# A two-layer hybrid kernel: retention by pairs of heads, and column sums that go through DRAM with each row in one piece

## The chip, the cores and the metric

The kernel runs on one core of a Trainium2 chip. The metric is the device time of one execution in microseconds. The engines spoken of are TensorE (PE in the profile, PEld its weight loads), VectorE (DVE), ScalarE (ACT), GpSimd (POOL), and SyncE (SP), which issues nearly all DMAs of this kernel in order from one queue.

## What is computed

Two models follow one another on a sequence of 512 positions of width 1024, each with two layers. Only the first model (block 1) holds code that is changed. One of its layers normalises the input, projects it, runs three branches (an RWKV-7 recurrence with 8 heads of 64, a retention with 4 heads, a spatial gating unit), gates and merges them, and ends with a gated feed-forward net. The parts of the reference that matter here:

```python
def retention_branch(p, cos, sin):
    q, k, v, g = jnp.split(p, ...)            # 4 heads, q and k of 64, v of 128
    q = rotary(q, cos, sin)
    k = rotary(k, cos, sin) * (RET_QK_DIM ** -0.5)
    ...
    y = (inner + cross)                       # (q k^T * decay) v, causal
    y = y * lax.rsqrt(jnp.mean(y * y, axis=-1, keepdims=True) + EPS)
    return y * jax.nn.silu(g)

def rwkv7_branch(...):
    ...
    kk = kk / jnp.maximum(jnp.sqrt(jnp.sum(kk * kk, axis=-1, keepdims=True)), 1e-12)
    y = rwkv7_scan(r, decay, k, v, kk, a)
    mean = jnp.mean(y, axis=-1, keepdims=True)
    var = jnp.mean(jnp.square(y - mean), axis=-1, keepdims=True)
    y = (y - mean) * lax.rsqrt(var + RW_GN_EPS) * lnx_g + lnx_b
    y = y + jnp.sum(r * k * r_k, axis=-1, keepdims=True) * v
    return y * g
```

## The kernel before, in words

Activations lie feature by position: a tile is 128 features by 512 positions. Each large product is done three times in a 32-bit round format (high times high, low times high, high times low, lines 170 to 172), so a tile of 128 outputs is 24 matmuls of 128x512. A weight block of 512 KB is loaded into one of two buffers (wraw, L157), split by ScalarE (whi, L161) and VectorE (wlo, L162) into one of two buffers each. The product gathers in one of two PSUM banks of pool pm, and VectorE takes it out (L428 in block 1). Pool pw has four banks (function P) for the chains of the recurrence, pool pf has two (function PF).

In a layer of block 1 the order of TensorE's work is written by a planner (class Plan, functions step and run). Threads are Python generators that issue instructions and then yield a step. Dense(cost) and TILE (cost 1.4) are dense work: the projections, six matmuls at a time, of thread rwkv_in (rank 1), then branches (retention, then the gating unit; rank 2), then gates1, the 24 gate tiles (rank 3), which fill whatever is left. Chain(cost, wait) says that the thread's next step is due after so many units of planned time, counted on all costs issued, and comes before dense work then. When nothing is left to issue, planned time jumps ahead. The orders of the other engines are made by the scheduler of the framework; within "with self.late()" an operation stands behind the last evacuation that was issued.

The chains around the change:

- rw_pair (one for each two heads f of the recurrence): psw and psa, two 64-row products (L477, L479); the squares of k are summed over each head (sums, "psk"), and after Chain(0.4, 13.0) kkr is made with the result (L527), then kr, bd (L530 to L533); psbon; after a further wait psA (L546) uses bd.
- rwkv_inverse on VectorE (L570 to L586), then two lanes of units (rw_unit) which work through four f and four chunks g; unit f > 1 is not begun until rw_final of f-2 has ended.
- rw_final: six small steps psz, then the sums "psmean" and, after Chain(0.4, 10.0), y plus mean (L742), "psq", Chain(1.6, 11.0), y times its norm (L755) and the last products (L756 to L758); the result is yrw[f].
- retention, for each pair f: q, k (with a rotation), v, and then for each head e of the pair in turn: a gate tile gt, the decay table dec by DMA (L800), and four steps j with a score of 512 - 128 j columns (pssc, L807; 64 rows of q and k: rows 0 to 63 for e = 0, 64 to 127 for e = 1), its product with the decay (pret, L810, VectorE) and psret (L812), which gathers the four. Both pssc and psret are in pool pf. After each head "psrn" sums its squares (norms), and ret_end multiplies (L825) when Chain 12.0 has passed.

The helper sums (L198 on) sums a tile over partitions for four chunks of 128 positions at once, into rows 32 g + i of a 128x128 tile (g the chunk, i the head of n), writes that whole tile to DRAM (sumd, L207, 64 KB) and reads it back n times (L209), each read a broadcast of one row, in four pieces of 128 numbers, to 128/n partitions.

After the plan the merge runs: for each tile of pbr a gate is read from DRAM (L934), the three branches are projected in the order of merge_order, VectorE multiplies (L940) and adds (L944). The first tile that uses yrw is the fifth.

Of the kernel before, what the change touches and what calls it, by code (L numbers as in the profile page):

```python
# [10 lines left out]
F32 = mybir.dt.float32  # L11
# [7 lines left out]
S = 512  # L19
# [36 lines left out]
def Chain(cost, wait):  # L56
    return Step(cost, wait, chain=True)
# [49 lines left out]
class Kern:  # L107
# [90 lines left out]
    def sums(self, x, sel, n, ps, out, fn):  # L198
# [7 lines left out]
        d = self.dp.tile([4, 32, 128], F32, name="sumd", tag="sumd", bufs=8)  # L206
        nc.sync.dma_start(d.rearrange("g r t -> (g r) t"), t)  # L207
        for i in range(n):
            nc.sync.dma_start(out[i * 128 // n:(i + 1) * 128 // n, :].rearrange("p (g t) -> p g t", g=4),  # L209
                              d[:, i][None].to_broadcast([128 // n, 4, 128]))  # L210
# [259 lines left out]
    def rw_pair(self, l, f, r, k, vt, m, lora, half):  # L470
# [52 lines left out]
        yield Chain(0.4, 13.0)  # L523
# [74 lines left out]
    def lane(self, l, i):  # L598

        while self.units:  # L600
# [9 lines left out]
            if not self.left[f]:  # L610
                self.plan.add(self.rw_final(l, f, self.states[f]), 0, 2.0)
# [98 lines left out]
    def rw_final(self, l, f, st):  # L710
# [6 lines left out]
        yield Chain(0.0, 1.0)  # L717
# [22 lines left out]
        yield Chain(0.4, 10.0)  # L740
# [12 lines left out]
        yield Chain(1.6, 11.0)  # L753
# [15 lines left out]
    def retention(self, l, win):  # L769
# [4 lines left out]
        for f in range(2):  # L774
# [18 lines left out]
            ws = self.stream([win[l, 22 + 2 * f], win[l, 23 + 2 * f]])  # L793
            for e in range(2):
                h = 2 * f + e
# [4 lines left out]
                dec = F(name="dec"); nc.sync.dma_start(dec, I["c_dec1"][h])  # L800
                yield Chain(0.0, 1.0)
                hs = slice(64 * e, 64 * e + 64)
                psy = self.PF(name="psret")
                for j in range(4):
                    n = S - 128 * j
                    ps = self.PF(name="pssc")
                    nc.tensor.matmul(ps[:, :n], lhsT=qk[1][hs, j * 128:(j + 1) * 128], rhs=qk[0][hs, j * 128:],  # L807
                                     start=True, stop=True)
                    p = T(name="pret")
                    nc.vector.tensor_tensor(p[:, :n], ps[:, :n], dec[:, :n], op=OP.mult)  # L810
                    yield Chain(0.3 + n / 1024, 3.2)
                    nc.tensor.matmul(psy[:, j * 128:], lhsT=vt[j // 2][:, j % 2, e * 128:(e + 1) * 128], rhs=p[:, :n],  # L812
                                     start=(j == 0), stop=(j == 3), skip_group_check=True)
                y = self.tile("Y", name="yret")
                sq = T(name="sqr")
                nc.scalar.activation(sq, psy, AF.Square)
# [1326 lines left out]
```

## Time and profile before

| | us |
|---|---|
| median of 3 runs | 3266.28 (3265.93 to 3267.68) |
| profiled execution | 3264.7 |
| its span, first to last instruction | 3263.0 |
| TensorE busy in the span | 3208.0 |
| VectorE busy | 2187.2 |
| ScalarE busy | 1362.0 |

The mean granted clock of TensorE is 0.996 of full speed. A busy time of TensorE counts each matmul from its start to a modelled end; they overlap in a pipeline, so that the distance between two starts is shorter than one's duration, and it is the distance that adds up to the span. A 32-bit matmul ("f32" with a 128x128 or 64x512 input that isn't split) stands in the profile as two records.

The first mixing stage of block 1 lies at about 20 to 500 us of the span with its merge from 487, the second at about 975 to 1450 with its merge from 1439.

### The profile page before, as it was taken

Reading aid. Unit: us, or ns where it says so; the run is one execution under the profiler, and the core shown is the slowest. Engines: PE = TensorE matmul, PEld = TensorE weight load, DVE = VectorE, ACT = ScalarE, POOL = GpSimd, SP = SyncE. Lnnn points to the kernel's source line nnn. Section 1 sums busy time; section 2 is a strip of 40 time slices with the busy share of each in tenths; the row PEclk is TensorE's granted clock in tenths of the full one; section 3 lists DMA queues with packets and bytes.
Section 4 is the critical chain, followed back from the end, with each engine's and each line's share of the span. In section 5 each row is a group of like instructions: output and inputs, shape, how many; then the busy total and the mean of one; then the engine's idle time right before and its main releaser. Section 6 shows DMA issues by size and latency. Waiting matters only on the chain.

```text
span 3263.0 us, 47497 instructions
## 1 busy us (share of the span) xinstructions
PE 3208.0 (98%) x17992; PEld 2574.7 (79%) x17992; DVE 2187.2 (67%) x4071; ACT 1362.0 (42%) x2442; POOL 124.9 (4%) x176
## 2 busy tenths in 40 slices
PE   8999999999999999999999999999999999999998
PEld 6787877888887787878888887877788888777777
DVE  6875656777537855656677456987666669866665
ACT  5533434444335333434444334344334443443343
POOL 0000000000000000000000000010003100100031
PEclk9999999999999999999999999999999999999999
DMA  4433245433433423245333436453355564534464
GB/s 148 132 99 88 85 137 178 127 102 97 139 107 108 130 82 96 81 156 180 101 97 98 150 122 206 143 148 109 118 194 187 175 174 139 152 109 124 151 213 145
DMA packets 199797, 434.75 MB, mean 133 GB/s; under 512 B 29833, under 2 KB 58633, under 8 KB 199569
## 3 DMA queue, kind: packets, MB, share of 16 engines
q1 hardware_dynamic: 197904, 429.62, 42.8%
q8 instruction: 142, 2.33, 0.3%
q0 software_dynamic: 512, 1.05, 0.1%
q10 hardware_dynamic: 1152, 1.05, 0.1%
q14 instruction: 87, 0.70, 0.1%
HBM read 339.05 MB, written 61.36 MB: 123 GB/s over the span
## 4 chain that ended last, share of the span: by engine, by line
PE 82%; DVE 8%; DMA 6%; issue 2%; ACT 2%; SPq 0%; POOL 0%; DVEq 0%; ACTq 0%; POOLq 0%
PE pm L170 21%; PE pm L172 21%; PE pm L171 21%; PE psy L1186 2%; PE pbr L170 2%; PE pbr L171 2%; PE pbr L172 2%; PE pspt L1176 2%; DVE wlo L162 2%; DMA rdw<-sumd 1%; DMA sqr<-sumd 1%; PE psl L1158 1%; PE psl L1159 1%; DMA sqk<-sumd 1%; DMA sumd<-sums 1%
## 5 line engine op out<-in xcount | busy, mean ns | idle before, releaser
L170 PE MATMUL pm<-shi,whi 128*128 128x512 f32 x3064 | 1227.0, 400 | 0.9 <-ACT whi L161 0.9
L172 PE MATMUL pm<-shi,wlo 128*128 128x512 f32 x3064 | 1202.2, 392 | 1.4 <-DVE wlo L162 1.4
L171 PE MATMUL pm<-slo,whi 128*128 128x512 f32 x3064 | 1201.0, 392 | 0.0
L161 ACT ACTIVATE whi<-wraw 128x1024 fp32r<-128x1024 f32 x480 | 508.4, 1059 | 887.0 <-PE pm L171 527.6
L162 DVE TENSOR_TENSOR wlo<-wraw,whi 128x1024 fp32r<-128x1024 f32 x480 | 588.1, 1225 | 198.4 <-ACT whi L161 193.1
L170 PEld LDWEIGHTS pm<-shi,whi 128*128 128x128 f32 x3064 | 577.3, 188 | 138.4 <-issue 26.9
L172 PEld LDWEIGHTS pm<-shi,wlo 128*128 128x128 f32 x3064 | 576.6, 188 | 125.8 <-DVE wlo L162 4.0
L171 PEld LDWEIGHTS pm<-slo,whi 128*128 128x128 f32 x3064 | 577.5, 188 | 111.7 <-issue 4.1
L428 DVE TENSOR_TENSOR ev<-pm,rb 128x512 f32<-128x512 f32 x138 | 94.7, 687 | 110.9 <-PE pm L172 110.1
L897 DVE TENSOR_TENSOR gate<-pm,rb 128x512 f32<-128x512 f32 x80 | 55.0, 688 | 127.3 <-PE pm L172 127.0
L170 PE MATMUL pbr<-shi,whi 128*128 128x512 f32 x288 | 113.8, 395 | 1.1 <-DVE gate L940 0.8
L170 PE MATMUL pm<-whi,shi 128*128 128x256 f32 x384 | 112.5, 293 | 1.3 <-DVE ev L428 1.3
L171 PE MATMUL pbr<-slo,whi 128*128 128x512 f32 x288 | 112.2, 390 | 0.0
L172 PE MATMUL pbr<-shi,wlo 128*128 128x512 f32 x288 | 112.2, 389 | 0.0
L171 PE MATMUL pm<-wlo,shi 128*128 128x256 f32 x384 | 108.9, 284 | 0.6 <-DVE wlo L162 0.6
L172 PE MATMUL pm<-whi,slo 128*128 128x256 f32 x384 | 108.9, 284 | 0.0
L940 DVE SCALAR_TENSOR_TENSOR gate<-gate,pbr 128x512 f32<-128x512 f32 x128 | 85.7, 683 | 29.1 <-PE pbr L172 28.5
L944 POOL TENSOR_TENSOR gate<-gate 128x512 f32<-128x512 f32 x48 | 78.0, 1626 | 590.5 <-DVE gate L940 335.6
L937 ACT ACTIVATE gate<-gate 128x512 f32<-128x512 f32 x128 | 76.2, 625 | 46.0 <-DMA gate<-gtd 40.1
L1143 ACT ACTIVATE p<-psl,st 128x256 f32<-128x256 f32 (+3 forms) x128 | 65.1, 512 | 60.4 <-DVE st L1141 50.9
L170 PEld LDWEIGHTS pm<-whi,shi 128*128 128x128 f32 x384 | 73.6, 192 | 3.8 <-DVE ev L428 1.7
L171 PEld LDWEIGHTS pm<-wlo,shi 128*128 128x128 f32 x384 | 73.8, 192 | 1.3 <-DVE wlo L162 1.1
(524 smaller groups left out, 4401.8 us busy)
## 6 DMA issues: line engine op xcount, KB each, us to landing
wraw<-in_w_gt SPq DMA_DIRECT2D x148, 512.0 KB, 3.6
wraw<-in_w_in SPq DMA_DIRECT2D x116, 512.0 KB, 3.6
wraw<-in_f_up SPq DMA_DIRECT2D x88, 512.0 KB, 3.5
gtd<-gate SPq DMA_DIRECT2D x116, 256.0 KB, 2.0
gate<-gtd SPq DMA_DIRECT2D x116, 256.0 KB, 4.2
wraw<-in_w_br SPq DMA_DIRECT2D x44, 512.0 KB, 3.7
wraw<-in_f_dn SPq DMA_DIRECT2D x44, 512.0 KB, 3.5
wraw<-in_w_out SPq DMA_DIRECT2D x32, 512.0 KB, 3.7
```

Source lines behind the costliest of these rows:

```text
L161: nc.scalar.activation(hi[:, :n], raw[:, :n], AF.Copy)
L162: nc.vector.tensor_tensor(lo[:, :n], raw[:, :n], hi[:, :n].bitcast(F32), op=OP.subtract)
L170: nc.tensor.matmul(ps, lhsT=lhs[0], rhs=rhs[0], start=first, stop=False, skip_group_check=skip)
L171: nc.tensor.matmul(ps, lhsT=lhs[0], rhs=rhs[1], start=False, stop=False, skip_group_check=skip)
L172: nc.tensor.matmul(ps, lhsT=lhs[1], rhs=rhs[0], start=False, stop=last, skip_group_check=skip)
L428: self.last = self.nc.vector.tensor_tensor(t, ps, self.rb, op=OP.mult)
L937: nc.scalar.activation(g, g, AF.Tanh, scale=0.5)
L940: nc.vector.scalar_tensor_tensor(g, g, 1.0, pb, op0=OP.add, op1=OP.mult)
L944: (nc.gpsimd if self.pre and n in self.cfg.get("pa", (1, 2, 3)) else nc.vector).tensor_tensor(g, g, acc[c], op=OP.add)
L1143: nc.scalar.activation(p[:, :w], l, AF.Exp, bias=st[:, 0:1], accum_out=st[:, 1:2])
L1176: nc.tensor.transpose(pt_[:, b * 128:(b + 1) * 128], ps[e][:, b * 128:(b + 1) * 128], self.ident)
L1186: nc.tensor.matmul(psy[64 * e:64 * e + 64, :], lhsT=vs[e][b], rhs=pts[e][:, b * 128:(b + 1) * 128], start=first and b == 0, stop=last and ...
```

## The change

Three things are changed together. In sums each row of the result gets a DRAM tile of its own, [4, 128], so there is one small write (4 partitions of 512 B) and one read (a broadcast of 2 KB in one piece) for each row i. In retention the two heads of a pair are worked together: both gate tiles first, then each step j has the scores of both heads one behind the other, both products with the decay, and in the next step both psret. The scores move from pool pf to pool pw, and so does psrn; dec moves from tag F to tag Y. The planned waits of some chains are other ones.

```diff
         t = self.ap.tile([128, 128], F32, name="sums", tag="sums", bufs=2)
         fn(t, ps)
-        d = self.dp.tile([4, 32, 128], F32, name="sumd", tag="sumd", bufs=8)
-        nc.sync.dma_start(d.rearrange("g r t -> (g r) t"), t)
+        d = self.dp.tile([n, 4, 128], F32, name="sumd", tag="sumd%d" % n, bufs=8)
         for i in range(n):
-            nc.sync.dma_start(out[i * 128 // n:(i + 1) * 128 // n, :].rearrange("p (g t) -> p g t", g=4),
-                              d[:, i][None].to_broadcast([128 // n, 4, 128]))
+            nc.sync.dma_start(d[i], t[i:128:32, :])
+        for i in range(n):
+            nc.sync.dma_start(out[i * 128 // n:(i + 1) * 128 // n, :],
+                              d[i].rearrange("g t -> (g t)")[None].to_broadcast([128 // n, S]))
...
-        yield Chain(0.4, 13.0)          # rw_pair, before kkr
+        yield Chain(0.4, 15.0)
...
-                self.plan.add(self.rw_final(l, f, self.states[f]), 0, 2.0)
+                self.plan.add(self.rw_final(l, f, self.states[f]), 0, 2.5)
...
-        yield Chain(0.0, 1.0)           # rw_final, before psz
+        yield Chain(0.0, 2.5)
...
-        yield Chain(0.4, 10.0)          # rw_final, behind psmean
+        yield Chain(0.4, 7.5)
...
-        yield Chain(1.6, 11.0)          # rw_final, behind psq
+        yield Chain(1.6, 8.5)
...
+            gts, decs = [], []
             for e in range(2):
-                h = 2 * f + e
                 gt = self.evac((yield from self.fm_steps(ws)), "F")
                 th = T(name="th")
                 nc.scalar.activation(th, gt, AF.Tanh, scale=0.5)
                 nc.vector.scalar_tensor_tensor(gt, th, 1.0, gt, op0=OP.add, op1=OP.mult)
-                dec = F(name="dec"); nc.sync.dma_start(dec, I["c_dec1"][h])
-                yield Chain(0.0, 1.0)
-                hs = slice(64 * e, 64 * e + 64)
-                psy = self.PF(name="psret")
-                for j in range(4):
-                    n = S - 128 * j
-                    ps = self.PF(name="pssc")
-                    nc.tensor.matmul(ps[:, :n], lhsT=qk[1][hs, j * 128:(j + 1) * 128], rhs=qk[0][hs, j * 128:],
+                dec = self.tile("Y", name="dec"); nc.sync.dma_start(dec, I["c_dec1"][2 * f + e])
+                gts.append(gt); decs.append(dec)
+                yield TILE if not e else Chain(1.4, 1.0)
+
+            psy = [self.PF(name="psret") for _ in range(2)]
+            for j in range(4):
+                n = S - 128 * j
+                ps = [self.P(name="pssc") for _ in range(2)]
+                for e in range(2):
+                    hs = slice(64 * e, 64 * e + 64)
+                    nc.tensor.matmul(ps[e][:, :n], lhsT=qk[1][hs, j * 128:(j + 1) * 128], rhs=qk[0][hs, j * 128:],
                                      start=True, stop=True)
-                    p = T(name="pret")
-                    nc.vector.tensor_tensor(p[:, :n], ps[:, :n], dec[:, :n], op=OP.mult)
-                    yield Chain(0.3 + n / 1024, 3.2)
-                    nc.tensor.matmul(psy[:, j * 128:], lhsT=vt[j // 2][:, j % 2, e * 128:(e + 1) * 128], rhs=p[:, :n],
+                p = [T(name="pret") for _ in range(2)]
+                for e in range(2):
+                    nc.vector.tensor_tensor(p[e][:, :n], ps[e][:, :n], decs[e][:, :n], op=OP.mult)
+                yield Chain(0.4 + n / 600, 3.6)
+                for e in range(2):
+                    nc.tensor.matmul(psy[e][:, j * 128:], lhsT=vt[j // 2][:, j % 2, e * 128:(e + 1) * 128], rhs=p[e][:, :n],
                                      start=(j == 0), stop=(j == 3), skip_group_check=True)
+            sqs, ys = [], []
+            for e in range(2):
                 y = self.tile("Y", name="yret")
                 sq = T(name="sqr")
-                nc.scalar.activation(sq, psy, AF.Square)
-                nc.vector.scalar_tensor_tensor(y, psy, 0.5, gt, op0=OP.mult, op1=OP.mult)
-                yield Chain(0.4, 3.0)
-                self.norms(sq, self.sel[:, 1], 1, self.PF([128, 128], "psrn"), bias=self.eps[:, 0:1], scale=1.0 / 128)
-                self.plan.add(self.ret_end(l, h, y, sq), 0, 12.0)
-                yield Dense(0.4)
+                nc.scalar.activation(sq, psy[e], AF.Square)
+                nc.vector.scalar_tensor_tensor(y, psy[e], 0.5, gts[e], op0=OP.mult, op1=OP.mult)
+                sqs.append(sq); ys.append(y)
+            yield Chain(0.8, 4.0)
+            for e in range(2):
+                self.norms(sqs[e], self.sel[:, 1], 1, self.P([128, 128], "psrn"), bias=self.eps[:, 0:1], scale=1.0 / 128)
+                self.plan.add(self.ret_end(l, 2 * f + e, ys[e], sqs[e]), 0, 10.0 + e)
+            yield Dense(0.8)
```

The words behind # in the five lines of planned waits are added here to say where each stands.

## Rows read from the trace of the kernel before

**Rows 1.** The page, first part: busy us of each engine, share, instructions.
```profile
PE 3208.0 (98%) x17992; PEld 2574.7 (79%) x17992; DVE 2187.2 (67%) x4071; ACT 1362.0 (42%) x2442; POOL 124.9 (4%) x176
```

**Rows 2.** Stretches: length, busy PE, PEld, DVE, ACT, POOL; PEclk, DMA share, GB/s.
```profile
20.00:500.00 480.00, 469.83 (x3317) 369.75 (x3316) 312.33 (x582) 200.96 (x410) 0.87 (x1) 1.00 0.35 108
975.00:1450.00 475.00, 465.87 (x3293) 367.02 (x3292) 308.62 (x572) 198.15 (x407) 0.63 (x1) 1.00 0.36 106
```

**Rows 3.** TensorE's waits, whole span: who waits for whom: total us, times, longest.
```profile
PE pbr L170 <- DVE gate L940: 6.6, 4, 2.9
PE psA L546 <- DVE kkr L533: 5.6, 5, 1.8
PE psam L651 <- ACT rhs L635: 3.6, 4, 1.2
...
PE psret L812 <- DVE pret L810: 2.3, 3, 1.0
```

**Rows 4.** Timeline of TensorE around scores: start, us, operation, shapes [idle before].
```profile
136.99 0.39 PE L172 MATMUL pm<-shi,wlo 128*128 128x512 f32 x1
...
137.67 0.39 PE L172 MATMUL pm<-shi,wlo 128*128 128x512 f32 x1
137.98 1.12 PE L807 MATMUL pssc<-ev 64*128 64x512 f32 x2
139.04 0.50 PE L170 MATMUL pm<-shi,whi 128*128 128x512 f32 x1
139.37 0.39 PE L171 MATMUL pm<-slo,whi 128*128 128x512 f32 x1
...
150.57 0.81 PE L812 MATMUL psret<-pret,vret 128*128 128x384 f32 x2
151.31 0.70 PE L807 MATMUL pssc<-ev 64*128 64x256 f32 x2
151.94 0.50 PE L170 MATMUL pm<-shi,whi 128*128 128x512 f32 x1
```

**Rows 5.** Timeline of TensorE at two 64-row products, psw and psa.
```profile
45.32 0.39 PE L172 MATMUL pm<-shi,wlo 128*128 128x512 f32 x1
45.64 0.69 PE L477 MATMUL psw<-mix,lora 64*128 64x512 f32 x1
45.65 0.69 PE L479 MATMUL psa<-mix,lora 64*128 64x512 f32 x1
...
46.70 0.50 PE L170 MATMUL pm<-shi,whi 128*128 128x512 f32 x1
```

**Rows 6.** The page's DMA issues: count, KB each, median us to landing.
```profile
sqr<-sumd SPq DMA_DIRECT2D x8, 256.0 KB, 8.3
...
rdw<-sumd SPq DMA_DIRECT2D x16, 128.0 KB, 5.7
...
cumb<-cumd SPq DMA_DIRECT2D x8, 256.0 KB, 3.7
```

**Rows 7.** Timeline of SyncE's queue behind the last psq of the first layer.
```profile
489.50 0.32 SPq L207 DMA_DIRECT2D sumd<-sums  x1
492.10 1.24 SPq L209 DMA_DIRECT2D rdw<-sumd  x2
```

**Rows 8.** Timeline of VectorE at the first layer's merge.
```profile
499.69 0.69 DVE L755 TENSOR_TENSOR y<-y,rdw 128x512 f32<-128x512 f32 x1 [4.33 <-DMA rdw<-sumd]
500.30 0.68 DVE L940 SCALAR_TENSOR_TENSOR gate<-gate,pbr 128x512 f32<-128x512 f32 x1
```

**Rows 9.** Timeline of TensorE at the same place.
```profile
501.13 0.63 PE L170 MATMUL pbr<-shl,whi 128*128 128x512 f32 x1 [2.91 <-DVE gate L940]
...
504.85 0.39 PE L170 MATMUL pbr<-shi,whi 128*128 128x512 f32 x1
```

**Rows 10.** The stretch 502 to 504, columns as in rows 2.
```profile
502.00:504.00 2.00, 2.00 (x6) 1.62 (x5) 1.93 (x4) 1.73 (x3) 0.00 (x0) 0.50 0.00 0
```

**Rows 11.** Timeline of VectorE at one kkr.
```profile
128.77 0.75 DVE L527 SCALAR_TENSOR_TENSOR kkr<-mix,vec,sqk 128x512 f32<-128x512 f32 x1 [3.30 <-DMA sqk<-sumd]
```

## The prediction

> **What bounds the kernel now.** I read the page's first part first: TensorE is busy for 3208.0 of 3263.0 us, VectorE for 2187.2 [rows 1]. So only two things can shorten this kernel: less TensorE time, or less of the 55 us in which it waits. Everything the change touches lies in block 1, which runs twice, so I next read the table of stretches for the two mixing stages: TensorE is busy 469.83 of 480 us and 465.87 of 475 us, VectorE about 65% of them [rows 2]. That leaves 10.2 + 9.1 us of idle time in these stages; cutting waits there can win no more. Third, the list of who waits for whom on TensorE [rows 3]: the largest named waits that belong to block 1 are psA on the last product of kkr (5.6 us in 5), psam on ACT L635 (3.6 in 4), psret on pret (2.3 in 3), and two of the four waits of pbr (2.9 us each, one at each layer's merge). The main term must therefore come out of TensorE's own time, and for that the timeline of TensorE must be read start to start: a busy TensorE isn't at its peak, and only the distance between starts tells what an instruction costs.
>
> **Scores by pairs.** Dense 128x512 matmuls start 0.227 us apart (136.99 to 137.67 in three steps). A score of 512 columns uses 64 of the 128 rows: the last dense start before it is at 137.67, it starts at 137.98, the next dense at 139.04 and the one after at 139.37 [rows 4]. So it takes 1.06 us, plus 0.08 before it (0.31 in place of 0.227) and 0.10 behind it (0.33 in place of 0.227): 1.24 us. The score of 256 columns behind a psret takes 151.94 - 151.31 = 0.63, and the psret of 384 columns before it takes 0.74, where 384 columns at the score's slope are 0.645: again 0.10 before and 0.10 behind [rows 4]. The slope is (1.06 - 0.63) / 256 = 1.68 ns a column, which gives 0.84 for 384 and 0.41 for 128 columns. With 0.18 to 0.20 for the two changes of shape the four scores of a head cost 1.24 + 1.03 + 0.83 + 0.60 = 3.70 us, of which about 2.13 is columns and 1.57 switching.
>
> What do two of them cost together? The trace of before has the very case: psw (rows 0 to 63) and psa (rows 64 to 127), both 64x512 in fp32, both into banks of the same pool. They start at 45.64 and 45.65, and the next dense matmul starts at 46.70: 1.06 us for both, with the same 0.32 before them [rows 5]. The second is free. In the changed kernel heads e=0 and e=1 stand on just these halves, and their two scores are issued in one loop with nothing between. So one of two heads' scores vanishes: 3.70 us for each pair, 2 pairs in a layer, 2 layers, **14.8 us**. The psret matmuls use all 128 rows and don't pair; their count is unchanged. Bounds: 8.5 if only columns are saved (4 x 2.13) and 15.5 if the norms, two of which now also share a place, save a switch as well (4 x 0.18).
>
> The Trainium skill (TensorEngine Tiling (Array Packing), Key Properties) says that tiles of different rows run in parallel and that a change of mode drains TensorE; both agree with these rows. The same page (Gotcha 1: PSUM Pressure) warns that row tiling needs more banks, and that speaks against this change; it is a rival below.
>
> **Banks of PSUM.** Today a score goes into pool pf (2 banks, with psret), and the recurrence's chains have pw (4 banks) to themselves. After, psret holds both pf banks for a whole pair, and the pairs of scores and psrn take pw. The trace shows what a wait for a bank of pw costs: psam on L635, 3.6 us in 4, 0.9 each [rows 3]. Of the 16 pairs of scores the 8 of f=1 run among the chains; if each met one such wait, 7.2 us; if none did, 0, and the four of now may also go. I take **2.5 us lost**, a third, because a score's bank is read by one VectorE instruction of 0.7 us or less and VectorE is a third idle.
>
> **psret and its decay table.** The planned wait goes from 3.2 to 3.6 for two products instead of one. Each pret stays one VectorE instruction; psret of e=0 (0.74 us for 384 columns, [rows 4]) covers that of e=1. The table of e=1 is fetched as late as today's, so one wait of 1 us in each pair may stay: between 2.3 us won [rows 3] and 1.7 lost (4.0 in place of 2.3); I take 0.
>
> **The sums through DRAM.** Today one 64 KB write and then, for two rows, two reads in pieces of 512 B. The reads land after 5.7 (rdw) and, with one row, 8.3 us (sqr); cumb, a broadcast of one 2 KB row to 128 partitions, moves as many bytes as sqr and lands after 3.7 [rows 6]. The new form is cumb's. I take 3.7 in place of 5.7 to 8.3, with 0 saved and 4.6 saved as ends. The write of a sum with two rows becomes two small ones, which costs SyncE one more issue of 0.32 us [rows 7] ahead of the weight loads that queue behind it. I take it at nothing: the two weight buffers stand for a tile of 24 dense matmuls, 24 x 0.227 = 5.5 us, ahead of TensorE, and the reads, 0.62 us to issue now [rows 7], have a quarter of the pieces; without that cover it would be 0.3 us a sum. The Trainium skill (DMA: Bandwidth & Descriptors, Specifications) puts line rate at 512 B and above; by that sentence alone the reads would gain nothing. The trace disagrees as far as it shows, 3.7 against 8.3.
>
> What this is worth is read where somebody waits for it.
> (a) *The merge.* VectorE sits from 495.4 to 499.69 in front of y L755 for rdw's read, and L940, which would free a bank of pm, is queued behind it until 500.30 [rows 8]. TensorE stops 2.91 us [rows 9], and then runs at half clock: granted 0.50 in 502 to 504, the level of 1.2 GHz [rows 10]. From 501.13 to 504.85 there are nine distances of matmuls, 3.72 us where 9 x 0.227 are 2.04 [rows 9]. So the stall costs 2.91 + 1.68 = 4.6 us, and the second layer has its twin: 9.2. After: writes issued at 489.5 and 489.8 land near 492.4, as the one of now has by 492.1 [rows 7]; reads issued by 492.8 land at 496.5; y to 497.2, L940 to 497.9, and the fifth tile was to start at about 498.06. Moreover psq itself comes earlier against the dense work: the planned waits behind mean and norm fall by 2.5 each (10 to 7.5, 11 to 8.5) while two grow by 0.5 and 1.5, and the gate tiles of retention now count 2.8 in the plan where they counted 0. So gates are left to fill the time behind psq. I take the whole **9.2 us**; ends 0 and 9.2.
> (b) *psA.* kkr is late because VectorE waits 3.30 us for sqk's read [rows 11]. The read comes some 2 us sooner and the planned wait is 2 longer; the longest wait of TensorE here is 1.8 [rows 3]. Of 5.6 us I take **4.5**; ends 0 and 5.6.
> (c) The shorter waits of rw_final (7.5, 8.5) and ret_end (10, 11 instead of 12) let VectorE reach y before the data, as now. Among dense tiles two banks and the same two weight buffers cover that for 5.5 us; without this cover it is the stall under (a), 4.6 us each. Nothing is taken.
>
> **Sum.** 14.8 + 9.2 + 4.5 - 2.5 = 26.0 us. The profiled execution took 3264.7 (span 3263.0), so 3238.7; the median of the runs, 3266.28, is 1.6 above it: 3240.3, and I say 3240. Edits that leave the number of ACT and VectorE instructions as it is (the decs in tag Y, the lists, the order of th and gt) cost nothing: VectorE has 35% to spare.
>
> **Rivals.**
> 1. *The reads don't get faster.* VectorE then waits at the merge as before, (a) is 0 and (b) gets only its two planned units, say 2: 14.8 + 2 - 2.5 = 14.3, 3252. For it: the reads queue behind 512 KB weight loads, which this change leaves alone. Against: cumb's 3.7 [rows 6]. This is the case that the Trainium skill's sentence on 512 B would give.
> 2. *PSUM pressure.* Each f=1 pair waits for a bank (7.2) and psA's wait stays: 14.8 + 9.2 - 7.2 = 16.8, 3249. For it: two of four pw banks go at once while two lanes use the pool. Against: in 955 us only 3.6 us of such waits [rows 2, 3].
> 3. *The pair doesn't overlap.* Then only 16 x 0.39 of switching is saved, 6.2, the sum 17.4, 3249. Rows 5 speak against it.
> 4. *Slower:* the scores of both heads wait on banks that VectorE frees late, because it sits in front of a sum's read. One stop of 2.9 us costs 4.6 with the half clock [rows 9]. Of 16 pairs 7 would have to stop so (32 us) to eat the 28.5 of (a), (b) and the scores; all 16 would give 3266 + 74 - 28.5, but 9, the likely lot if lanes and sums coincide, 41, give 3279. For it: TensorE's order is fixed, so a late bank stops all; against: no stop among the chains is now above 1.8 us.
>
> **How the numbers follow.** Forecast 0.65 (3232 to 3247); rival 1 0.13; rival 2 0.09; rival 3 0.03; rival 4 0.05; a mixture in which little is left (planned order worse for the chains) 0.05. Upper end of the gain: 15.5 + 9.2 + 5.6 + 2.3 = 32.6, 3233; lower: 8.5 + 4.6 - 7.2 = 6, 3260. The range 3231 to 3256 takes in rivals 1 to 3 and leaves out rival 4 and part of the mixture. A measurement of this kernel can tell about 0.2%, 6.5 us, from no change: faster by more 0.89, within 0.06, slower 0.05.
>
> **What would show it.** In the new profile pssc of e=0 and e=1 start within 0.02 us and the next dense start follows 1.06 us (512 columns) later; the reads of sumd land in about 4 us; no wait of pbr near 2.9 and no stretch at 0.50 behind it; psA's waits under 1.5 us in all. The prediction is wrong if pairs of pssc start one behind the other, or if new waits of pssc, psh or psu for banks add up to more than 8 us.

## The result, and the profile after

The changed kernel takes 3234.34 us (median of 4 runs, 3233.67 to 3236.9) against 3266.98 of the kernel before on the same chip: ratio 0.9898, 95% interval 0.988 to 0.9915. The profiled execution took 3233.67 us with a span of 3232.0, so 31.0 us less than that of before. The forecast of 3240 had the size nearly right, but, as the experiments show, two of its terms were off by more than 10 us each, in opposite directions.

The page of the changed kernel, busy time of the engines, beside [rows 1]:

```profile
PE 3185.4 (99%) x17992; PEld 2567.0 (79%) x17992; DVE 2184.4 (68%) x4071; ACT 1359.0 (42%) x2438; POOL 124.9 (4%) x176
```

TensorE is busy 22.6 us less; the rest of the 31.0 is idle time that has gone. Its waits in the changed kernel, beside [rows 3] (who waits for whom, total us, times, longest):

```profile
PE psam L653 <- ACT rhs L637: 2.9, 4, 1.3
PE psam L653 <- DVE y L760: 2.6, 2, 1.4
...
PE psz L724 <- DVE cc L726: 2.3, 2, 1.2
...
PE pbr L170 <- DVE gate L951: 1.8, 2, 1.2
PE psz L724 <- DVE am L658: 1.7, 1, 1.7
PE psA L548 <- DVE kkr L535: 1.6, 4, 0.5
...
PE psmean L202 <- DVE am L658: 1.1, 2, 0.6
```

pbr fell from 6.6 to 1.8 us, psA from 5.6 to 1.6, and psret isn't in the list any more. The two stops of 2.9 us at the merges of block 1 are gone altogether: what is left of pbr stands at 3085 us and later, in the second model, whose code is the same in both kernels. New or longer are the lines of the recurrence: psam on y, psz and psmean make, together with pst (1.2) and psam on rhs (3.6 before), 11.8 us. VectorE's waits for rows of sums are listed next, first before (50.2 us in all), then in the changed kernel:

```profile
DVE y L755 <- DMA rdw<-sumd: 19.9, 6, 4.3
...
DVE yret L825 <- DMA sqr<-sumd: 12.2, 4, 6.4
...
DVE y L742 <- DMA cc<-sumd: 9.8, 4, 4.0
...
DVE kkr L527 <- DMA sqk<-sumd: 8.3, 6, 3.3
```

```profile
DVE yret L836 <- DMA sqr<-sumd: 1.7, 2, 1.2
DVE y L744 <- DMA cc<-sumd: 1.5, 2, 1.0
```

TensorE around two pairs of scores (start, us, operation), beside [rows 4]. The first group has the scores of both heads and nothing else:

```profile
140.46 1.13 PE L812 MATMUL pssc<-ev 64*128 64x512 f32 x4
141.52 0.50 PE L170 MATMUL pm<-shi,whi 128*128 128x512 f32 x1
...
152.62 1.45 PE L819 MATMUL psret<-pret,vret 128*128 128x384 f32 x4
154.00 0.70 PE L812 MATMUL pssc<-ev 64*128 64x256 f32 x4
154.63 0.50 PE L170 MATMUL pm<-shi,whi 128*128 128x512 f32 x1
```

Four records (two matmuls of 512 columns) take 141.52 - 140.46 = 1.06 us, exactly what one took before. Two of 256 columns take 0.63, as one did.

The first layer's merge: all engines, only the steps of the chain of the last psq, beside [rows 7 and 8]:

```profile
468.85 0.43 PE L202 MATMUL psq<-rdw,sel 128*32 128x128 f32 x8
...
470.72 1.10 SPq L209 DMA_DIRECT2D sumd<-sums  x2
472.97 1.14 SPq L211 DMA_DIRECT2D rdw<-sumd  x2
...
477.82 0.68 DVE L757 TENSOR_TENSOR y<-y,rdw 128x512 f32<-128x512 f32 x1
```

Nothing stands in brackets behind the last line: VectorE no longer waits for rdw. Between psq and the merge, which starts at 477.01, 30 dense matmuls of the gate tiles stand now; before, the merge began right behind psq. Stretches of the changed kernel (columns as in [rows 2]): the 100 us from the merge on, and the one place in the two layers where the clock still falls, with the stop in front of it:

```profile
480.00:580.00 100.00, 100.00 (x443) 82.81 (x442) 66.12 (x87) 42.32 (x56) 0.00 (x0) 1.00 0.58 179
...
300.00:302.00 2.00, 0.65 (x7) 0.65 (x8) 2.00 (x6) 1.12 (x4) 0.00 (x0) 0.86 0.50 125
302.00:304.00 2.00, 2.00 (x8) 1.38 (x7) 2.00 (x5) 1.30 (x2) 0.00 (x0) 0.50 0.34 137
```

```profile
301.36 0.64 PE L653 MATMUL psam<-kr,kkr 64*64 64x128 f32 x4 [1.41 <-DVE y L760]
```

At the merge the clock stays at 1.00. At 300 us TensorE stands 1.41 us in front of a psam and then runs 2 us at 0.50 (1.2 GHz), while VectorE is busy 2.00 of 2.00 us.

**One table for all runs.** To compare the kernels I split TensorE's time in the two mixing layers with their merges (each from its first dense matmul to the feed-forward net's norm). "Idle" is the sum of the gaps that the timeline shows in front of instructions. "Half clock" is busy time times (1 - granted clock), summed over slices of 2 us in which the clock was below 0.97. "Work" is what remains. The ratio is to the kernel before as it was timed beside each run on the same chip; its medians there were 3266.98 to 3271.96.

```
                          work    idle   half clock  sum      median us (ratio)
before                   1145.5   23.2      4.8     1173.5    3266.98
sums alone               1142.4    3.1      0.0     1145.5    3239.71 (0.9917)
pairs alone              1127.4   46.3     15.5     1189.2    3283.65 (1.0052)
planned waits alone      1142.6   40.2     19.4     1202.2    3294.91 (1.0088)
sums + pairs             1124.7   20.3      8.9     1153.9    3247.91 (0.9941)
sums + planned waits     1140.3    2.2      0.0     1142.5    3236.98 (0.9897)
pairs + planned waits    1126.0   44.7     21.1     1191.8    3282.92 (1.0043)
all three (changed)      1126.2   13.9      1.5     1141.6    3234.34 (0.9898)
```

The rest of the program, outside these two layers, took 2089.5 us before and 2090.4 after, and up to 2096.3 in other runs though nothing in it differs: up to 7 us of a difference between medians can lie there (the waits of pbr in the second model, 0.8 to 5.2 us, are a part of it), and for small differences I go by the layers.

### The profile page after: what moved, and what is told of

It reads as the page before. It is cut to its first block, busy times and chain, and to the rows that moved or that the text cites. A ratio compares the mean times of both kernels' runs of the same rounds, so it can differ in the third digit from the quotient of the medians.

```text
span 3232.0 us, 47541 instructions
## 1 busy us (share of the span) xinstructions
PE 3185.4 (99%) x17992; PEld 2567.0 (79%) x17992; DVE 2184.4 (68%) x4071; ACT 1359.0 (42%) x2438; POOL 124.9 (4%) x176
## 2 busy tenths in 40 slices
DMA packets 179252, 432.28 MB, mean 134 GB/s; under 512 B 29480, under 2 KB 32968, under 8 KB 179024
## 4 chain that ended last, share of the span: by engine, by line
PE 88%; DVE 7%; ACT 2%; DMA 1%; issue 1%; POOL 0%; SPq 0%; DVEq 0%; ACTq 0%; POOLq 0%
PE pm L170 23%; PE pm L172 22%; PE pm L171 22%; PE pbr L170 2%; PE psy L1197 2%; PE pbr L171 2%; PE pbr L172 2%; PE pspt L1187 2%; DVE wlo L162 1%; PE psl L1169 1%; PE psl L1170 1%; ACT whi L161 1%; DVE R L586 1%; DVE tmp L584 1%; PE psg L669 0%
## 5 line engine op out<-in xcount | busy, mean ns | idle before, releaser
L951 DVE SCALAR_TENSOR_TENSOR gate<-gate,pbr 128x512 f32<-128x512 f32 x128 | 85.7, 682 | 26.1 <-PE pbr L172 25.5
```

What stands on the lines that cost most here:

```text
L951: nc.vector.scalar_tensor_tensor(g, g, 1.0, pb, op0=OP.add, op1=OP.mult)
```

## The experiments

**The three parts, alone and in twos.** The edit of each is the part of the diff above that its name says: sums (the helper sums), pairs (retention), planned waits (the five yields and the delay of rw_final; the retention's own yields go with the pairs).

> The sums' part alone (one small write and one read of 2 KB rows for each row), retention and planned waits as before. My theory: the reads land some 2 to 4 us sooner, so at both merges VectorE no longer sits 4.3 us in front of y L755, the 2.9 us stop of TensorE and the half clock behind it go (9.2 us for two layers), and psA's waits fall from 5.6 to about 3: 9 to 12 us faster, 3255 to 3258. Rival, the merge is cured by the planned waits (gates left behind psq) and not by the reads: under 3 us faster, with a wait of pbr near 2.9 still in the profile.

Measured: 3239.71 us (3238.37 to 3240.73), ratio 0.9917 (0.9902 to 0.9932): 27.4 us. VectorE's waits for rows of sums are gone altogether. From the table: idle time 20.1 us less, half clock 4.8 less, work 3.1 less. At the merges of block 1 pbr doesn't wait at all (the 3.0 us of pbr that its list has stand at 2433 and 3097 us, in the second model), and no stretch of the layers is at 0.50: it is the reads that cure the merge, not the planned waits. So the sums alone are worth twice the 13.7 that I gave them; both expectations were too small.

> Retention by pairs alone (with its own planned waits), sums and the other waits as before. My theory: TensorE's work falls by 14.8 us (one of two scores free), the waits of psret (2.3) go, new bank waits of about 3 come; the merge's stop stays if only the sums matter there: 13 to 16 us faster, 3250 to 3253. Rival, the pairs are worth more because the longer plan also leaves gates at the merge: 20 us or more, and no wait of pbr near 2.9.

Measured: 3283.65 us (3281.76 to 3286.0), ratio 1.0052 (1.0037 to 1.0067): 16.5 us slower, against both expectations. TensorE, then VectorE, with pairs alone:

```profile
PE psmean L202 <- DVE am L656: 13.3, 2, 6.7
...
PE psam L651 <- DVE cc L724: 7.0, 2, 3.5
```

```profile
DVE yret L834 <- DMA sqr<-sumd: 31.7, 7, 6.3
```

The work falls by 18.1 us, as a pair should bring; idle time and half clock grow by 33.8. The two retention results of a pair now come one behind the other, and VectorE sits 31.7 us in front of their slow reads (12.2 before); what TensorE waits for (am, cc, and rhs with 9.8 us) are products of VectorE and ScalarE in the recurrence. No line names pssc. How much of the 33.8 is the slow reads is told by sums + pairs below.

> The five planned waits of the recurrence's chains alone. My theory: psA's waits fall by 2 units each, 4 of 5.6 us, and gates are left behind psq so that the merge's stop shrinks, while VectorE now reaches y of L742 and L755 about 2.5 us further ahead of data that comes as late as before: between 3 and 10 us faster. Rival, the shorter waits belong to the faster reads and hurt without them: VectorE's waits for sumd grow from 50 us to over 60 and the time does not fall.

Measured: 3294.91 us (3293.2 to 3297.89), ratio 1.0088 (1.0071 to 1.0105): 27.8 us slower. Waits of TensorE and of VectorE:

```profile
PE pst L625 <- ACT cc L707: 9.2, 2, 4.9
```

```profile
DVE yret L825 <- DMA sqr<-sumd: 32.5, 6, 9.0
DVE y L755 <- DMA rdw<-sumd: 29.0, 8, 6.2
```

The rival holds: VectorE's waits for these rows go from 50.2 to 72.9 us. For y of L755, whose planned wait was cut, the reading is that a planned wait shorter than the data's way doesn't bring the data; it puts VectorE in front of it earlier, with everything behind it. That isn't the whole of it: yret, which rose most (12.2 to 32.5), has the planned wait of before in this run, and y of L742, whose wait was cut too, fell from 9.8 to 4.9. Why yret meets its reads so much worse here wasn't traced. Idle time and half clock come to 59.6 us, 31.6 more than before.

> Sums and pairs together, the five planned waits of the recurrence's chains undone. My theory, parts add up: what is missing to the whole change is what the planned waits are worth on top of faster reads, some 3 us for psA and little at the merge: 3236 to 3240. Rival, the parts overlap (sums and planned waits both cure the merge): within 2 us of the whole change, 3233 to 3236.

Measured: 3247.91 us (3245.29 to 3249.38), ratio 0.9941 (0.9926 to 0.9956): 8 us slower than the sums alone, although the work is 17.7 less. Both expectations were too low. Of TensorE's waits the line with the longest stops, the second of these two stops in the timeline, and the stretches there:

```profile
PE psam L653 <- DVE cc L726: 6.7, 2, 3.5
```

```profile
1250.37 0.69 PE L653 MATMUL psam<-kr,kkr 64*64 64x128 f32 x4 [3.21 <-DVE cc L726]
```

```profile
1248.00:1250.00 2.00, 0.00 (x0) 0.00 (x0) 2.00 (x6) 0.00 (x0) 0.00 (x0) 0.95 0.61 238
1250.00:1252.00 2.00, 1.63 (x9) 1.21 (x10) 1.94 (x8) 0.30 (x1) 0.00 (x0) 0.50 0.02 4
```

TensorE stands 3.21 us while VectorE is busy without a gap; behind it the clock is 0.50. psz of one lane's rw_final and psam of both lanes stand within 6 us of one another there. Here the reads are fast (VectorE waits 9.6 us for them in all), so this is a loss of the pairs' new order, not of the reads. And it is the larger part: with fast reads the pairs add 26.1 us of idle time and half clock, with slow ones 33.8.

> The whole change without the pairs: sums and the five planned waits, retention head by head as before. Theory A: the planned waits are worth their 13.6 us of the last comparison only because they move the two lanes of the recurrence out of the places where the pairs bring them together; without pairs there are only 3 us of TensorE's waits left to win in the stages (sums alone), so 3236 to 3244, and the pairs are worth 3 to 10 us on top of sums and planned waits. Theory B: the planned waits cost, as they did alone, because they make VectorE meet reads too early: over 3244.

Measured: 3236.98 us (3233.86 to 3237.58), ratio 0.9897 (0.9881 to 0.9914). Without pairs, the kernel is as fast as the whole change. Idle time in the layers is 2.2 us, with no slice below full clock; with pairs work is 14.1 less, and idle and half clock are 13.2 more. In the changed kernel as it stands the pairs bring next to nothing: 2.6 us between the medians, 0.9 in the layers, where theory A had 3 to 10.

> The changed kernel with the sums of before: a 64 KB write, reads in four pieces a row; pairs and the five planned waits as changed. It ends the set of eight (pairs, sums, planned waits, each on or off). Theory L (the slow rows of sums are what the shorter planned waits and the pairs run into): pairs alone cost 16.5 and planned waits alone 27.8, and the two together cost 25 to 45 us against the kernel before, so 3292 to 3312; VectorE waits 50 us or more for the rows read back, and TensorE's idle time in two layers is over 40 us. Theory C (the planned waits were made for the pairs and bring them to pay even with slow sums): below the kernel before, 3250 to 3266.

Measured: 3282.92 us (3279.29 to 3284.94), ratio 1.0043 (1.0029 to 1.0056): 14.0 us slower than before. The theory that the planned waits make the pairs pay even with slow sums has fallen; the other one named the right cause and gave 25 to 45, too much. The five planned waits, which cost 27.8 us alone, cost next to nothing here: with slow sums and pairs the layers go from 1189.2 to 1191.8 by them. With pairs and planned waits in place, the sums' new form is worth 1.0043 - 0.9898, some 48 us.

**Does the pair run side by side?** In this kernel one head's psret stands between the two scores, for j = 1 to 3; j = 0 stays a pair.

```diff
-            for j in range(4):
+            p = None
+            for j in range(5):
                 n = S - 128 * j
...
-                for e in range(2):
+                for e in (1, 0):
                     hs = slice(64 * e, 64 * e + 64)
-                    nc.tensor.matmul(ps[e][:, :n], lhsT=qk[1][hs, j * 128:(j + 1) * 128], rhs=qk[0][hs, j * 128:],
-                                     start=True, stop=True)
+                    if p:
+                        m = n + 128
+                        nc.tensor.matmul(psy[e][:, j * 128 - 128:], lhsT=vt[(j - 1) // 2][:, (j - 1) % 2, e * 128:(e + 1) * 128],
+                                         rhs=p[e][:, :m], start=(j == 1), stop=(j == 4), skip_group_check=True)
+                    if ps:
+                        nc.tensor.matmul(ps[e][:, :n], lhsT=qk[1][hs, j * 128:(j + 1) * 128], rhs=qk[0][hs, j * 128:],
+                                         start=True, stop=True)
...
```

> The changed kernel with the two heads' score matmuls taken apart for blocks 1 to 3 of each pair of heads: one head's product with the values of the block before stands between them, so that the two 64-row matmuls cannot lie beside each other; block 0 stays a pair. Nothing is left out. Theory O (the pair costs the time of one because the two matmuls run beside each other): the stages of retention get longer by the scores' columns of blocks 1 to 3, (384 + 256 + 128) columns at 2.4 GHz times 4 cycles a column = 1.28 us a pair, and by some 0.39 us for each of the three more changes between 64 and 128 rows, 2.4 us for each of 4 pairs: 9 to 10 us more, 3243 to 3245. Theory N (the pair saves only because there are fewer changes of rows and planned steps): 3 to 5 us more at most, 3237 to 3239.

Measured: 3244.11 us (3240.55 to 3244.24), ratio 0.9922 (0.9906 to 0.9938), 9.8 us more than the changed kernel. Its timeline at j = 2, to be read against the changed kernel's at 152.62:

```profile
153.94 0.81 PE L815 MATMUL psret<-pret,vret 128*128 128x384 f32 x2
154.68 0.70 PE L818 MATMUL pssc<-ev 64*128 64x256 f32 x2
155.30 0.91 PE L815 MATMUL psret<-pret,vret 128*128 128x384 f32 x2
156.15 0.70 PE L818 MATMUL pssc<-ev 64*128 64x256 f32 x2
156.77 0.50 PE L170 MATMUL pm<-shi,whi 128*128 128x512 f32 x1
```

The same four matmuls take 156.77 - 153.94 = 2.83 us here and 154.63 - 152.62 = 2.01 there: 0.82 more, of which 0.62 is the second score (156.77 - 156.15) and 0.20 one more change from 128 rows to 64 and back, as [rows 4] had it (0.08 + 0.10). For j = 1 it is 3.69 against 2.65, for j = 3 1.98 against 1.38; 2.46 us for a pair of heads, 9.8 for four of them. The work in the two layers grew by 8.5 us (1134.7 against 1126.2). That the second score is free is shown. Of the 9.8 between the medians, some 3 us lie outside the layers in the profiled execution, so the match of the medians alone would not show it as well.

**Are the pairs' new waits those of two lanes that stand in one place?** Scores stay in pool pw; the second lane starts later, and gets 4 units more behind each wait for rw_final:

```diff
-            self.plan.add(self.lane(l, i), 0, 2.0 * i)
+            self.plan.add(self.lane(l, i), 0, 6.0 * i)
...
             if f > 1 and not self.ended[f - 2]:
+                held = True
                 yield Chain(0.0, 1.0)
                 continue
+            if held and i:
+                held = False
+                yield Chain(0.0, 4.0)
+                continue
```

> The changed kernel with the two lanes kept apart: lane 1 begins 6 planned units behind lane 0 (2 before) and comes 4 units later out of each wait for rw_final. Theory A: the new waits of the pairs (psam on ACT L637, psam on DVE y L760, psz on cc, psmean on am: 13.9 us of idle time in groups, and the half clock behind some of them) stand where both lanes issue psam, two banks each, in one place; apart, at least half of them go: 3222 to 3230. Theory B: they come from the scores, which take two of the four pw banks: the waits stay, and the longer chain costs a little: 3233 to 3240.

Measured: 3225.11 us (3224.53 to 3226.31), ratio 0.9863 (0.9847 to 0.9879): 9.2 us faster than the changed kernel (8.6 in the layers), and the fastest kernel of this study. In the layers: work 1123.0, idle 6.7, half clock 3.3, sum 1133.0. The largest wait of the chains that is left:

```profile
PE psz L730 <- DVE cc L732: 4.0, 2, 2.2
```

psam isn't in the list any more, though the scores still take banks of the same pool. So the banks that the scores hold were not what psam waited for. The changed kernel's own times say the same: in its first layer the last score starts at 246.20 us, and the stops at 301.36 (psam), 310.21 (psz), 339.53 (psmean) and 397.30 (pst) come more than 50 us behind it; the one at 178.53 (psam) comes 17 us behind the last score of the first pair of heads. What psam waits for is still a bank of pool pw, as far as the code tells: its inputs are made long before, and rhs and cc, which end most of its waits, are read out of other tiles of that pool (pst and psz). But these are the recurrence's own tiles. Is the later start good by itself? The same edit on sums + planned waits, without pairs:

> New sums and new planned waits without the pairs (3236.98 on the chip), and in it the later start of the second lane (6.0 units in place of 2.0, and 4 units more behind each wait for the end of a chunk's work) that brought the changed kernel to 3225.1. Theory A (the pairs save 14.8 us of TensorE's work, and what hid this was the waits of two lanes that stand in one place): with the lanes apart in both, the pairs are worth 10 to 15, so this kernel is at 3235 to 3240. Theory B (the pairs are worth nothing here, the later start is worth 9 us by itself): 3226 to 3229.

Measured: 3244.24 us (3243.05 to 3245.57), ratio 0.9926 (0.991 to 0.9941). Neither expectation: without pairs the later start costs 7.3 us. In the layers work is 1140.1, idle 10.0, half clock 1.5.

```profile
PE psam L659 <- DVE am L664: 3.8, 2, 1.9
```

So the start of the second lane is no remedy as such; it is a setting that fits one order of the work. With lanes apart the pairs are worth 3244.24 - 3225.11 = 19.1 us (17.1 of it work), with the start as it was 2.6 (3236.98 against 3234.34). What is shown is that the work saved is there in every order, and that the waits which eat it depend on where the two lanes stand. Why the pairs bring the lanes to a bad place with the old start, I didn't trace in the planner.

**Which part of the sums' new form is it?** First, the 64 KB write of before with reads in one piece:

```diff
-        d = self.dp.tile([n, 4, 128], F32, name="sumd", tag="sumd%d" % n, bufs=8)
-        for i in range(n):
-            nc.sync.dma_start(d[i], t[i:128:32, :])
+        d = self.dp.tile([32, 4, 128], F32, name="sumd", tag="sumd", bufs=8)
+        nc.sync.dma_start(d.rearrange("r g t -> g r t"), t)
```

> The changed kernel with the sums' write as before, 64 KB of all 128 rows in one DMA, but to a tile in which each row is in one piece, so that the reads stay broadcasts of 2 KB. If the reads' pieces are what matters: within 3 us of the changed kernel, 3231 to 3238. If the small write matters as well: 3240 or more, with VectorE's waits for sumd's reads above 10 us.

Measured: 3242.54 us (3240.57 to 3244.32), ratio 0.9916 (0.9899 to 0.9933). In the layers it is 1146.3 against 1141.6 of the changed kernel, and VectorE waits 12.2 us for these rows against 3.2. So the second expectation holds, by little. Second, small writes and reads described as four pieces of 128 numbers:

```diff
-            nc.sync.dma_start(out[i * 128 // n:(i + 1) * 128 // n, :],
-                              d[i].rearrange("g t -> (g t)")[None].to_broadcast([128 // n, S]))
+            nc.sync.dma_start(out[i * 128 // n:(i + 1) * 128 // n, :].rearrange("p (g t) -> p g t", g=4),
+                              d[i][None].to_broadcast([128 // n, 4, 128]))
```

> The changed kernel with its small writes, but the reads issued as four pieces of 512 B for each partition, as before. If the pieces matter: the reads land in 5 to 8 us again, VectorE's waits for sumd go from 3 us back to some 60 with the shortened planned waits, and the time rises by 25 us or more, to 3260 or above. If small pieces cost nothing (the write was the matter): 3233 to 3238.

Measured: 3238.18 us (3235.78 to 3239.88), ratio 0.990 (0.9881 to 0.992). Its packets are the changed kernel's to the last one, 179252 with 32968 under 2 KB: the four pieces lie end to end and are fetched as one. It tested nothing and is a second run of the changed kernel, 3.8 us above the first; 2.3 of that in the layers. That bounds what the 4.7 of the run before can mean. Third, the pieces truly apart, 512 B between them:

```diff
-        d = self.dp.tile([n, 4, 128], F32, name="sumd", tag="sumd%d" % n, bufs=8)
+        d = self.dp.tile([n, 4, 2, 128], F32, name="sumd", tag="sumd%d" % n, bufs=8)
         for i in range(n):
-            nc.sync.dma_start(d[i], t[i:128:32, :])
+            nc.sync.dma_start(d[i, :, 0, :], t[i:128:32, :])
         for i in range(n):
-            nc.sync.dma_start(out[i * 128 // n:(i + 1) * 128 // n, :],
-                              d[i].rearrange("g t -> (g t)")[None].to_broadcast([128 // n, S]))
+            nc.sync.dma_start(out[i * 128 // n:(i + 1) * 128 // n, :].rearrange("p (g t) -> p g t", g=4),
+                              d[i, :, 0, :][None].to_broadcast([128 // n, 4, 128]))
```

> The changed kernel with one thing different: in DRAM the four 512-byte pieces of each row of sums lie 512 bytes apart, so that no read of a row can be one piece of 2 KB; writes stay small (16 KB at the most wanted rows), order of TensorE's work is that of the changed kernel. In the run where only the order in the read's description was changed, the number of packets under 2 KB was that of the changed kernel (32968), so it did not test this. Theory P (the length of the read's pieces sets the landing): packets under 2 KB go back up to some 58000, VectorE waits again for the rows it reads back from DRAM, 25 us or more in all (before 50, changed kernel 3), and the time is 10 to 35 us above the changed kernel's 3234. Theory W (what counts is that 16 or 32 KB are written instead of 64 KB): VectorE's waits for these rows stay under 8 us and the time is within 5 us of 3234. The run with the 64 KB write and one-piece reads came 8 us above 3234, with waits of 12 us: if both hold in part, this one lies at 3242 to 3255.

Measured: 3234.46 us (3233.17 to 3237.17), ratio 0.9897 (0.9878 to 0.9916): the changed kernel's time, as theory W has it. (A row is 4 partitions of 512 B, so the small writes are 2 KB each, not the 16 or 32 KB of the expectation.) The page's packets, of this kernel and then of the changed one:

```profile
DMA packets 194612, 432.28 MB, mean 134 GB/s; under 512 B 29480, under 2 KB 53448, under 8 KB 194384
```

```profile
DMA packets 179252, 432.28 MB, mean 134 GB/s; under 512 B 29480, under 2 KB 32968, under 8 KB 179024
```

The pieces are there, and they cost nothing here. Neither part of the old form costs much by itself (4.7 us in the layers at most); both together cost 48 us. The way of the last pair of retention's sums in layer 2 shows how near the edge each comes. Timelines of the issue of the two reads of 256 KB and of the products that wait for them (in the last also TensorE's stop behind them), of the changed kernel, of the pieces apart, of the 64 KB write, and of both together (pairs + planned waits):

```profile
1198.01 0.80 SPq L211 DMA_DIRECT2D sqr<-sumd  x2
1201.54 1.38 DVE L836 TENSOR_TENSOR yret<-yret,sqr 128x512 f32<-128x512 f32 x2 [0.52 <-DMA sqr<-sumd]
```

```profile
1198.20 0.93 SPq L211 DMA_DIRECT2D sqr<-sumd  x2
1201.74 0.69 DVE L836 TENSOR_TENSOR yret<-yret,sqr 128x512 f32<-128x512 f32 x1 [0.51 <-DMA sqr<-sumd]
...
1203.74 0.69 DVE L836 TENSOR_TENSOR yret<-yret,sqr 128x512 f32<-128x512 f32 x1 [1.31 <-DMA sqr<-sumd]
```

```profile
1202.47 1.09 SPq L210 DMA_DIRECT2D sqr<-sumd  x2
1206.38 0.69 DVE L835 TENSOR_TENSOR yret<-yret,sqr 128x512 f32<-128x512 f32 x1 [2.03 <-DMA sqr<-sumd]
...
1207.55 0.69 DVE L835 TENSOR_TENSOR yret<-yret,sqr 128x512 f32<-128x512 f32 x1 [0.49 <-DMA sqr<-sumd]
```

```profile
1237.84 0.92 SPq L209 DMA_DIRECT2D sqr<-sumd  x2
1244.25 0.69 DVE L834 TENSOR_TENSOR yret<-yret,sqr 128x512 f32<-128x512 f32 x1 [3.67 <-DMA sqr<-sumd]
...
1248.18 0.69 DVE L834 TENSOR_TENSOR yret<-yret,sqr 128x512 f32<-128x512 f32 x1 [3.24 <-DMA sqr<-sumd]
...
1249.13 0.69 PE L651 MATMUL psam<-kr,kkr 64*64 64x128 f32 x4 [4.78 <-DVE cc L724]
```

From the first read's issue to the first product: 3.53, 3.54, 3.91 and 6.41 us; to the second product 4.2 at most (VectorE goes straight on), 5.54, 5.08 and 10.34. The Trainium skill (DMA: Bandwidth & Descriptors, Specifications) has 512 B as enough for full rate: the pieces 1 KB apart agree with it nearly, 5.54, the pieces of before don't, 10.34. Two things set these apart: the pieces of one row lay 16 KB apart in DRAM, and they came out of one 64 KB write. Which of the two makes the pieces slow, or whether it takes both, stays open; no run here has 16 KB between the pieces with small writes.

## Why the prediction was right and wrong

**Scores by pairs: right, a little small.** Forecast 14.8 with bounds 8.5 and 15.5. The work column gives, from each kernel without pairs to its twin with them, 18.1 (alone), 17.7 (with sums), 16.6 (with planned waits), 14.1 (with both) and 17.1 (lanes apart): mean 16.7. The second score costs no time (1.06 us for both), as [rows 5] said. The excess over 14.8 wasn't taken apart: the retention's norms stand together now, and the planner's groups are fewer (114 places in a layer where other work breaks into the dense matmuls, against 119 with sums + planned waits). psret, put at 0, won its 2.3.

**Sums: right that the reads come sooner, half in size.** (a) and (b) came nearly as said: the two stops at the merges and the half clock behind them are gone, psA fell from 5.6 to 1.6 where 4.5 of gain was taken and the sign was under 1.5. The reason given, reads in one piece, is half of it: pieces of 512 B behind small writes are as good. But the sums alone brought 27.4, not 13.7. The step that failed is to price them "where somebody waits" and to look only at TensorE's list for that. VectorE's own list had 50.2 us in front of these reads, and behind each such wait stand all its other products. One such place of the kernel before, VectorE and then TensorE:

```profile
1285.53 0.69 DVE L825 TENSOR_TENSOR yret<-yret,sqr 128x512 f32<-128x512 f32 x1 [6.42 <-DMA sqr<-sumd]
```

```profile
1286.61 0.71 PE L678 MATMUL psu<-rhs,tt 128*128 128x128 f32 x4 [1.53 <-DVE rhs L674]
```

The product rhs, for which psu waits, stands right behind yret in VectorE's order. So the psam, psu, psret and evacuation waits, for which the row names another releaser, went too, and with them the half clock behind psA's wait (4.8 us in all before, of which the forecast counted the merge's 2 x 1.68). The 10.2 + 9.1 us read from [rows 2] as the most that shorter waits can win were too little as well: the sums alone took out 20.1 us of idle time and 4.8 of half clock, which is hidden in the busy time there.

**(c), "Nothing is taken": wrong in both directions.** The planned waits cost 27.8 us with the old sums and give 12.3 in the layers with sums and pairs (1153.9 to 1141.6), 3.0 with sums alone. The cover that I named, two banks and two weight buffers, is for dense tiles; the chains of the recurrence have none. Even for dense tiles it isn't always enough: with pairs + planned waits two of them wait 12.6 us in all for L428, VectorE's evacuation.

**PSUM banks: the size and the place were wrong.** I took 2.5 with an end of 7.2 for banks that scores hold. With pairs idle time and half clock grew by 26.1 us (sums to sums + pairs) or 13.2 (without pairs to all three). With the pairs, pssc, psrn and psret wait nowhere, save for one pssc of 0.42 us in pairs + planned waits, and with the scores in the same pool the lanes' later start took psam's wait away. The condition "new waits of pssc, psh or psu over 8 us" never struck, since the loss lay at psam, psz, pst and psmean, 11.8 us where 5.2 were before: I had named the signs at the instructions that the change touches, and it came to others that share VectorE and the pool with them. The Trainium skill (TensorEngine Tiling (Array Packing), Gotcha 1: PSUM Pressure) warns of the banks of row tiles; here the one wait of a score, 0.42 us, is all that the runs show of it.

**The sum** was within 5 us of the profiled execution (26.0 forecast, 31.0 measured) in good part by luck: the sums' missing 14 us and the lanes' unexpected 11 to 24 us lie on different sides. Of the 31.0, the sums account for nearly all. Of the rivals, the first (reads not faster) is what the slow reads' kernels show, and it comes out worse than 3252: 3283 with the same pairs and planned waits. The fourth, slower for late VectorE, is near the mechanism of that kernel, though what stops is psam and dense tiles and not the scores: its idle time and half clock are 65.8 us. The fast reads are what sets the changed kernel apart from it.

## What to carry to other kernels

Before pricing a faster read, sum the waits of the engine that consumes it, not only those of the bound engine: what is queued behind the consumer waits too. Split the bound engine's time into work, idle time and half clock; a change that saves work can lose it in the next column, and the three parts of this one have signs that depend on one another (planned waits: 27.8 us slower alone, 13.6 faster as the last part). Shorten planned waits only after the data's way is short, and when work is taken out of an order by hand or planner, look again at where parallel chains meet.

## What the hardware showed

TensorE fell to 1.2 GHz behind stops shorter than the 2.91 us of [rows 9]: behind one of 1.41 us in the changed kernel the granted clock was 0.50 in the slice from 302 to 304, and behind one of 1.79 us in front of psA, before, it was 0.50 from 1028 to 1030. The length of the stop alone doesn't tell: before, psA's stop of 1.50 us at 74.68 has no stretch below full clock behind it. In the kernels with many stops the half clock comes to 15 to 21 us, a third to a half as much as the stops themselves.

At the place shown, two reads of 256 KB, each a broadcast of one row of 2 KB, take at most 4.2 us from the first issue to the second product; the same bytes in pieces of 512 B that lie 16 KB apart, behind 64 KB writes, take 10.3, and in pieces 1 KB apart behind writes of 2 KB they take 5.5.
